# Seven block products for seven more pairs, and a setup that is split between two stages

## The chip, the cores and the metric

The kernel runs on one core of a Trainium2 chip. A core has five engines, each with its own instruction stream: PE (TensorE, matrix products), DVE (VectorE) and ACT (ScalarE) for elementwise work, POOL (GpSimd) and SP (SyncE), which mostly issue transfers here; ACT issues some too. Sixteen DMA engines move the data. The metric is device microseconds of one execution, the median of three runs. In the profile PE is the matmul stream and PEld the weight loads that run beside it.

## The reference

A trunk of two layers over 512 tokens with 1024 channels, all in float32. Each layer is: half a SwiGLU feed-forward, a token mixer, half a SwiGLU feed-forward, each behind an RMSNorm and with a residual. The mixer of the first layer is a chunked state-space scan (SSD), that of the second a diagonal state-space model (S5).

```python
def rmsnorm(x, g):
    xf = xf * lax.rsqrt(jnp.mean(xf * xf, axis=-1, keepdims=True) + NORM_EPS)
    return xf.astype(x.dtype) * g

def swiglu(h, w_in, w_out):            # FFN_DIM = 2816
    gate, up = jnp.split(h @ w_in, 2, axis=-1)
    return (jax.nn.silu(gate) * up) @ w_out

def s5_mixer(h, b_re, ..., glu_w, glu_b):
    step = jnp.exp(log_step)[:, None]
    lam_bar = jnp.exp(lam * step)                      # 64 groups x 64 complex states
    b_bar = ((lam_bar - 1.0) / lam)[..., None] * lax.complex(b_re, b_im)
    ...  # states[t] = lam_bar * states[t-1] + b_bar u[t];  y = Re(c states) + d u
    val, gate = jnp.split(gelu(y) @ glu_w + glu_b, 2, axis=-1)
    return val * jax.nn.sigmoid(gate)
```

So there are six stages in order: `f1_0`, `ssd`, `f2_0`, `f1_1`, `s5`, `f2_1`, and a final norm.

## The kernel before

The residual stream lies transposed in SBUF as eight tiles `xT[d]` of 128 channels by 512 tokens. Float32 accuracy comes from splitting each operand in a high and a low half (`H`, `L` of the activations, `whi`, `wlo` of the weights): a product is three matmuls, hi x hi, hi x lo and lo x hi (`proj`, L371 to L376). ACT casts the high half (L365), DVE subtracts for the low one (L367). Weights come through a ring of four staging tiles `wst` and rings of three `whi` and `wlo`.

**Feed-forward stages** (`ffn`, from L590). The 22 pairs of a gate and an up tile (128 hidden channels each) are worked in three parts, pairs 0 to 7, 8 to 14 and 15 to 21 (`PARTS`). Each part ends with eight output products, one for each `xT[d]`, which is updated at once. The norm's factor is applied to the products, so `H` and `L` hold the input times the gain.

A *plain* pair is two `proj` of eight k-steps with 512 columns. A *block* pair (class `Seven`, L385) uses a seven-product scheme for 2 x 2 blocks: the two halves of the tokens are the columns, and even and odd 128-channel tiles of the input together with gate and up give the blocks. It needs sums and differences of weight tiles, formed partly by accumulating DMAs on POOL's queue (L391, L392) and partly on DVE (L431, L435), and four *forms* of the activations (`forms`, L319, one call for each two input tiles), sums and differences of the scaled `xT` tiles, split in halves again. Each product is 4 k-steps x 3 matmuls of 256 columns, all at L445. Stages `f1_1` and `f2_1` use block pairs throughout, `f2_0` three plain pairs and then block pairs, `f1_0` only plain pairs.

**The S5 setup** (`s5_setup`, from L1051) has nothing to do with the data: it computes from the S5 parameters the operators `d_H` and `d_P`, and tables of rotation angles `d_t`, and leaves them in HBM for the S5 stage. It runs inside `f1_0`: `ffn` calls the next entry of a list `fill` after each pair and each output product (46 places). `lam` does the exponentials and powers in pieces, doubles the angle (`usq`), `tables(i)` builds eight tables of 8 groups each by doubling, `ops(i)` the operators of four groups, `ops_pe(i)` products on PE for two such steps. All its tiles lie in the pool `pre0`, freed when `f1_0` ends. Every table has 128 partitions, real and imaginary rows with a sign that differs between the two halves of the partitions.

**The order.** In `f1_0` all engines' orders come from a planner that simulates time; instructions inside `keep_in_program_order` keep their order among each other, and `issue_after(x)` puts those of a block behind `x`. In the other feed-forward stages PE keeps the written order (`manual_schedule(engines=MAN)`). `paced` is such a kept transfer on SP's queue. Each queue works strictly in order.

**The S5 stage** (`s5_stage`) loads per block of eight groups `U`, `opH`, `tb` (a table) and two `opP` tiles. The 16 `opP` tiles come through a ring of six (`hx`), loaded by SP at L1409. `swap_in` and `swap_out` exchange the two halves of the partitions on ACT. The gated product at the end (`glu_w`, `load_w` on POOL's queue) and the first block pairs of `f2_1` (`seven_ahead`) overlap the last scans.

## Time and profile before

| what | us |
|---|---|
| median of three runs (1981.59 to 1982.64) | 1982.21 |
| profiled execution | 1983.18 |
| its span | 1981.4 |
| PE busy | 1964.9 |
| DVE busy | 1524.8 |
| ACT busy | 944.7 |
| POOL busy | 237.1 |

The profiled execution's own time is 1.78 us more than the span that its instructions cover. The stages lie in the span at about 0 to 390 (`f1_0`), 390 to 807 (`ssd`), 807 to 1153 (`f2_0`), 1153 to 1496 (`f1_1`), 1496 to 1637 (`s5`) and from there to the end (`f2_1`). The granted clock is 0.999 of the full one. A row of a group reads: line, engine, operation, written tile <- read tiles, shapes, count | busy us, mean ns of one | idle time of the engine before them and what ended it. A row of the timeline or the chain begins with the start and the length in us.

### The profile page before, as it was taken

The numbers are of one execution on the slowest core, as the hardware profiler recorded it, in microseconds if no ns is written. First come the engines' busy times: TensorE is split into PE (matmuls) and PEld (weight loads), VectorE is DVE, ScalarE is ACT, GpSimd is POOL, SyncE is SP. The second block draws the span as 40 slices with busy tenths as digits, with TensorE's granted clock in tenths as the row PEclk, the third lists the DMA queues.
The fourth block names the chain that finished last, engine by engine and source line by source line (L and its number), as shares of the span: only waits on it lengthen the run. The fifth ranks groups of instructions, "written<-read, shape, count | busy, mean of one in ns | idle before, by whom it ended". The sixth has DMA issues, their size and how long they took to land.

```text
span 1981.4 us, 32556 instructions
## 1 busy us (share of the span) xinstructions
PE 1964.9 (99%) x12669; PEld 1735.2 (88%) x12669; DVE 1524.8 (77%) x2630; ACT 944.7 (48%) x1472; POOL 237.1 (12%) x261
## 2 busy tenths in 40 slices
PE   9999999999999999999999999999999999999998
PEld 7888888888888888898989899898988789999897
DVE  6898986888888678875858887585868668667685
ACT  5322233565565355552525555352557446435363
POOL 1000000012111110111202111120201112111110
PEclk9999999999999999999999999999999999999999
DMA  7444564544333422684858767585998348667572
GB/s 191 107 138 146 155 194 128 138 126 133 114 105 113 116 88 76 134 185 107 182 122 176 187 142 172 115 177 121 185 265 284 89 105 174 160 136 167 122 158 86
DMA packets 503994, 288.28 MB, mean 145 GB/s; under 512 B 47808, under 2 KB 489312, under 8 KB 503840
## 3 DMA queue, kind: packets, MB, share of 16 engines
q1 hardware_dynamic: 408384, 217.02, 38.7%
q0 software_dynamic: 73728, 55.28, 16.9%
q10 hardware_dynamic: 21728, 13.91, 2.5%
q8 instruction: 99, 1.62, 0.3%
q14 instruction: 55, 0.45, 0.1%
HBM read 264.60 MB, written 21.04 MB: 144 GB/s over the span
## 4 chain that ended last, share of the span: by engine, by line
PE 93%; DVE 3%; DMA 2%; ACT 1%; issue 1%; ACTq 0%; SPq 0%; DVEq 0%
PE mm L445 31%; PE mm L374 18%; PE mm L375 18%; PE mm L376 18%; DMA wst<-in_s_glu_w_dram 1%; PE aux L959 1%; PE aux L901 1%; PE aux L1564 1%; PE aux L951 0%; DMA xt<-in_x_dram 0%; PE aux L852 0%; PE aux L376 0%; PE aux L375 0%; PE aux L374 0%; DMA opP<-d_P 0%
## 5 line engine op out<-in xcount | busy, mean ns | idle before, releaser
L365 ACT CAST whi<-wst 128x1024 fp32r<-128x1024 f32 (+2 forms) x220 | 216.9, 991 | 412.7 <-PE mm L375 275.4
L374 PE MATMUL mm<-hH,whi 128*128 128x512 f32 x776 | 306.3, 395 | 0.0
L375 PE MATMUL mm<-hL,whi 128*128 128x512 f32 x776 | 302.4, 390 | 0.0
L376 PE MATMUL mm<-hH,wlo 128*128 128x512 f32 x776 | 302.4, 390 | 0.0
L445 PE MATMUL mm<-hx,whi 128*128 128x256 f32 x1512 | 280.8, 283 | 0.0
L367 DVE TENSOR_TENSOR wlo<-wst,whi 128x1024 fp32r<-128x1024 f32 (+2 forms) x220 | 253.7, 1155 | 29.2 <-ACT whi L365 27.2
L374 PE MATMUL mm<-ah,whi 128*128 128x512 f32 x648 | 252.7, 391 | 0.0
L375 PE MATMUL mm<-al,whi 128*128 128x512 f32 x648 | 252.5, 390 | 0.0
L376 PE MATMUL mm<-ah,wlo 128*128 128x512 f32 x648 | 251.9, 390 | 0.0
L445 PEld LDWEIGHTS mm<-hx,whi 128*128 128x128 f32 x1512 | 236.4, 192 | 0.7
L410 DVE TENSOR_TENSOR wlo<-wst,whi 128x1024 fp32r<-128x1024 f32 x126 | 154.3, 1224 | 91.8 <-ACT whi L407 88.7
L445 PE MATMUL mm<-hx,wlo 128*128 128x256 f32 x756 | 214.1, 283 | 0.2 <-DVE wlo L410 0.2
L445 PE MATMUL mm<-hL,whi 128*128 128x256 f32 x672 | 190.3, 283 | 0.5 <-DVE hL L272 0.3
L445 PE MATMUL mm<-hH,wlo 128*128 128x256 f32 x672 | 190.6, 284 | 0.2
L445 PE MATMUL mm<-hH,whi 128*128 128x256 f32 x672 | 190.3, 283 | 0.0
L376 PEld LDWEIGHTS mm<-hH,wlo 128*128 128x128 f32 x776 | 145.6, 188 | 30.6
L374 PEld LDWEIGHTS mm<-hH,whi 128*128 128x128 f32 x776 | 145.7, 188 | 30.4 <-issue 0.7
L375 PEld LDWEIGHTS mm<-hL,whi 128*128 128x128 f32 x776 | 145.8, 188 | 29.5 <-issue 0.2
L407 ACT CAST whi<-wst 128x1024 fp32r<-128x1024 f32 x126 | 131.6, 1045 | 37.3 <-PE mm L375 29.6
L445 PEld LDWEIGHTS mm<-hx,wlo 128*128 128x128 f32 x756 | 145.1, 192 | 0.4 <-DVE wlo L410 0.4
L376 PEld LDWEIGHTS mm<-ah,wlo 128*128 128x128 f32 x648 | 121.6, 188 | 25.3
L375 PEld LDWEIGHTS mm<-al,whi 128*128 128x128 f32 x648 | 121.7, 188 | 24.8 <-issue 0.4
(499 smaller groups left out, 3936.3 us busy)
## 6 DMA issues: line engine op xcount, KB each, us to landing
wst<-in_ffn_w_in_dram SPq DMA_DIRECT2D x175, 512.0 KB, 4.4
wst<-in_ffn_w_out_dram SPq DMA_DIRECT2D x56, 448.0 KB, 4.2
wst<-in_ssd_in_proj_dram SPq DMA_DIRECT2D x48, 512.0 KB, 3.9
wst<-in_ffn_w_out_dram SPq DMA_DIRECT2D x39, 512.0 KB, 4.1
wx<-in_ffn_w_in_dram SPq DMA_DIRECT2D x63, 256.0 KB, 3.2
wx<-in_ffn_w_in_dram POOLq DMA_DIRECT2D x63, 256.0 KB, 6.9
wst<-in_ffn_w_in_dram POOLq DMA_DIRECT2D x63, 256.0 KB, 5.0
dec<-d_cs POOLq DMA_DIRECT2D x16, 512.0 KB, 5.3
```

The costliest lines, as they stand in the source:

```text
L365: S.copy(hi, st)
L367: V.tensor_tensor(lo, st, hi.bitcast(F32), op=OP.subtract)
L374: PE.matmul(ps, hi[:, k], H[k], start=first and k == 0, stop=False)
L375: PE.matmul(ps, hi[:, k], L[k], start=False, stop=False)
L376: PE.matmul(ps, lo[:, k], H[k], start=False, stop=last and k == n - 1)
L407: self.pin(S.copy(hi, st))
L410: self.pin(V.tensor_tensor(lo[:, c], st[:, c], hi[:, c].bitcast(F32), op=OP.subtract))
L445: PE.matmul(ps, w_[:, j], b_, start=nm not in self.open, stop=False, skip_group_check=True)
L901: PE.matmul(pst[c], st["bt"][:, c * 128:(c + 1) * 128], st["wx"][:, c], start=True, stop=True)
L959: PE.matmul(py[e][hh * 64:(hh + 1) * 64, s], st["dtx"][:, c, k0:k0 + 64], M[:, hh, s], start=True, stop=True)
L1564: PE.matmul(py[i, h][e * 64:e * 64 + 64, g * 128:g * 128 + 128], l[:, h * 4 + g], out_ops(i + e, h)[:, g, w:w + 128], start=first and g == ...
```

## The change

1. **`f1_0`:** pairs 15 to 21 become block pairs. Since `xT` has been updated by then, `forms` gets a way (`split_only`) that adds the halves `H` and `L` again in place of reading `xT`. The four forms are made at output products 1 to 4 of the second part, the first block pair's transfers are issued at product 5 and its splits come at product 7. From pair 15 on, PE keeps the written order. The forms' tiles (pools `hx0`, `h10`) take the memory of the setup's pool, which is closed at output product 1.
2. **The setup in two parts:** in `f1_0` it is squeezed from 45 entries into 24 (pairs 0 to 14, the first eight output products and one more). The angle is left in a small tile `turn`. The doubling and the tables move to `f2_0` (`s5_tables`, 11 entries at places 4 to 35).
3. **Halved tables:** the angle tile holds 32 groups on each half of the partitions, so a table build makes two tables at once (four builds in place of eight, on half-width operands while doubling). Both halves of a stored table are the same now, written by four transfers on ACT's queue in place of one on POOL's; the sign goes into one of the two copies of `swap_in` and `swap_out`. The builds have two `t_cs` buffers.
4. **S5 tiles:** the last two `opP` tiles are loaded early, in kept order, into `wst` tiles; the first gated weight's transfer is issued early and its split held behind the last scan; the first block pairs of `f2_1` issue their transfers behind the last clearing of a state tile on POOL.
5. Some setup tiles share or leave tags (`p_E` takes the place of `p_B2` before it, `p_ks` its own), and the last `ks` stores go to POOL's queue.

```diff
-        def forms(self, j, fp, hp):
+        def forms(self, j, fp, hp, split_only=False):
...
+            if split_only:
+                he, le, ho, lo_ = [t_[i].bitcast(F32) for i in (e, o) for t_ in (self.H, self.L)]
+                V.tensor_tensor(a[:, lo], he[:, lo], le[:, lo], op=OP.add)
+                V.tensor_tensor(a[:, hi], a[:, lo], he[:, hi], op=OP.subtract)
+                V.tensor_tensor(a[:, hi], a[:, hi], le[:, hi], op=OP.subtract)
+                V.scalar_tensor_tensor(b[:, lo], ho[:, hi], -1.0, a[:, hi], op0=OP.mult, op1=OP.subtract)
+                V.tensor_tensor(b[:, lo], b[:, lo], lo_[:, hi], op=OP.subtract)
...
         for f in range(a, b):
             u.normed = normed
-            n = Seven(pr, w_in, f + 1, fp, pin) if f + 1 < b else None
+            with ExitStack() as behind:
+                if f == 0 and pr.after:
+                    behind.enter_context(tc.issue_after(pr.after.ins))
+                n = Seven(pr, w_in, f + 1, fp, pin) if f + 1 < b else None
...
+        if tail:
+            plain = PARTS[-1][0]
...
+                if tail and a == plain:
+                    seven = True
+                    by_hand.enter_context(tc.manual_schedule(engines=MAN))
...
+                    if tail and b == plain:
+                        if d == 1:
+                            hp = tail()
+                        if d in (1, 2, 3, 4):
+                            formed = pr.forms(d - 1, fp, hp, split_only=True)
+                        elif d == 5:
+                            u = Seven(pr, w_in, b, fp)
+                        elif d == KD - 1:
+                            with tc.issue_after(formed.ins):
+                                u = seven_first(pr, w_in, b, fp, u)
...
-            ER = pp.tile([128, 8, 64], F32, tag="p_wh", name="p_ER", bufs=2)
-            EI = pp.tile([128, 8, 64], F32, tag="p_wh", name="p_EI", bufs=2)
+            E_ = pp.tile([128, 2, 8, 64], F32, tag="p_B2", name="p_E", bufs=1)
+            ER, EI = E_[:, 0], E_[:, 1]
...
-            G.dma_start(d_t[i], cs)
...
-                nc.scalar.dma_start(ov[q, :, 4 * i:4 * i + 8, 128 + 16 * q:256], ks[:, :, 0:128 - 16 * q])
+                (G if i == 14 else nc.scalar).dma_start(ov[q, :, 4 * i:4 * i + 8, 128 + 16 * q:256], ks[:, :, 0:128 - 16 * q])
...
+        fill = [masks, both(rows, one, lambda: load_c(0), lambda: load_c(1)), both(one, lambda: load_c(2), b(0, 1)),
+                both(one, b(2, 3)), both(one, lambda: c_cols(0), b(4, 5)), both(one, lambda: c_cols(1), b(6, 7)),
+                both(one, lambda: c_cols(2), swap_b), both(steps.pop(0), lambda: c_cols(3), zero.pop(0))]
+        while steps:
+            f = steps.pop(0)
+            fill.append(both(f, zero.pop(0)) if zero and len(fill) % 2 else f)
+        assert not zero and len(fill) == 23
+        return fill + [lambda: ops_pe(14)]
+
+    def s5_tables(tp):
+        c, s = s5["turn"][:, 0], s5["turn"][:, 1]
...
+            for _ in range(3):
+                usq(c, s)
+            yield
+            for j in range(6):
+                V.tensor_copy(UC[:, j], c)
+                V.tensor_scalar(US[:, 0, j], s, -1.0, None, op0=OP.mult)
+                V.tensor_copy(US[:, 1, j], s)
+                if j < 5:
+                    usq(c, s)
+                if j == 2:
+                    yield
+            yield
+            for i in range(4):
+                cs = tp.tile([128, 2, 8, 64], F32, name="t_cs", bufs=2)
...
+                    if j == 3:
+                        yield
+                for h in range(2):
+                    for e in range(2):
+                        nc.scalar.dma_start(s5["t"][i + 4 * h][64 * e:64 * e + 64], cs[64 * h:64 * h + 64])
+                yield
...
     def out_ops(i, h):
         if (i, h) not in s5_out:
+            src = s5["P"][:, i * 8 + h * 4:i * 8 + h * 4 + 4]
+            if i >= KD - 2 and h:
+                P_ = wpool.tile([128, KD, 128], F32, name="wst", bufs=4).rearrange("p (g a) n -> p g (a n)", g=4)
+                paced(P_, src)
+            else:
...
-                    pin(S.copy(fl(z2)[64:128, c], p[0:64, c]))
+                    pin(S.activation(fl(z2)[64:128, c], p[0:64, c], AF.Copy, scale=-1.0))
...
                     if m == 2:
+                        for e in range(2):
+                            out_ops(KD - 2 + e, 1)
                         glu_k(0)
...
-            p0, w0 = aux_ps(), load_w(glu_cols(2 * NR), KD, eng=G)
+            p0, st0 = aux_ps(), fetch_w(glu_cols(2 * NR), KD, G)[0]
...
+            w0 = behind_states(split_w, st0, KD)
+            nxt.after = st[KD - 1]["cleared"]
...
                 if d == KD - 1 and nxt.kind == "wino":
-                    seven_ahead(nxt)
+                    with tc.issue_after(nxt.after.ins):
+                        seven_ahead(nxt)
...
+                    tabs, fill = s5_tables(tp), [lambda: None] * 46
+                    for n in (4, 10, 12, 14, 18, 20, 24, 26, 28, 33, 35):
+                        fill[n] = tabs.pop(0)
+                    ffn(pr, wi[L], wo[L], nxt, fill=fill, hp=hp)
```

161 lines of the change are left out of this document (85 added, 76 removed).

## The prediction

> **What bounds the kernel now.** I read the page's busy table and chain first, then windows by stage, then single rows.
>
> ```profile
> span 1981.4 us, 32556 instructions
> PE 1964.9 (99%) x12669; PEld 1735.2 (88%) x12669; DVE 1524.8 (77%) x2630; ACT 944.7 (48%) x1472; POOL 237.1 (12%) x261
> PE 93%; DVE 3%; DMA 2%; ACT 1%; issue 1%; ACTq 0%; SPq 0%; DVEq 0%
> ```
>
> TensorE never rests for long, and it carries 93% of the chain that ended last. So time leaves this kernel only where a TensorE instruction leaves its stream, or where one of the few idle gaps closes. All else decides only whether that gain is kept. DVE is the one to watch; the windows follow the first stage (0 to 390), its part before and after 268 us, the third stage (807 to 1149), and that stage's last seven pairs and last outputs. The columns are length, then busy time and count of PE, PE's weight loads, DVE, ACT and POOL, clock, DMA share and GB/s.
>
> ```profile
> 0.00:18.00 18.00, 15.56 (x84) 12.46 (x85) 9.87 (x25) 10.13 (x17) 9.00 (x24) 1.00 0.95 267
> 18.00:42.00 24.00, 24.00 (x140) 19.03 (x139) 17.89 (x39) 13.74 (x20) 0.18 (x1) 1.00 0.60 160
> 42.00:60.00 18.00, 18.00 (x81) 14.90 (x80) 11.60 (x18) 7.19 (x10) 0.00 (x0) 1.00 0.38 104
> 60.00:100.00 40.00, 40.00 (x179) 33.10 (x178) 36.99 (x128) 12.29 (x18) 0.00 (x0) 1.00 0.46 106
> 100.00:225.00 125.00, 125.00 (x573) 103.11 (x572) 115.63 (x339) 35.37 (x45) 3.77 (x7) 1.00 0.50 146
> 0.00:268.00 268.00, 265.56 (x1264) 217.44 (x1265) 228.15 (x606) 89.94 (x124) 13.48 (x33) 1.00 0.55 151
> 807.00:1149.00 342.00, 342.00 (x2326) 316.18 (x2325) 255.84 (x386) 164.78 (x247) 51.58 (x41) 1.00 0.68 152
> 1039.00:1109.00 70.00, 70.00 (x581) 69.87 (x580) 60.12 (x87) 39.94 (x61) 15.25 (x12) 1.00 0.80 169
> 1120.00:1150.00 30.00, 29.72 (x138) 24.73 (x137) 28.99 (x51) 19.19 (x33) 2.57 (x2) 1.00 0.51 121
> ```
>
> From 60 to 225 us DVE is busy 152.62 of 165 us (92.5%), yet TensorE waits for nothing. DVE can be driven that hard here without a stall.
>
> **Seven pairs as block products.** A plain pair is 2 x 8 x 3 = 48 matmuls of 512 columns; a block pair is 7 x 4 x 3 = 84 of 256 columns. The prices are two rows of the plain stream (51 matmuls apart) and one chain row of a whole block pair.
>
> ```profile
> 44.67 0.39 PE L376 MATMUL mm<-hH,wlo 128*128 128x512 f32 x1
> 56.23 0.39 PE L376 MATMUL mm<-hH,wlo 128*128 128x512 f32 x1
> 1877.35 10.08 PE mm L445 x84
> ```
>
> 11.56 / 51 = 0.2267 us, so a plain pair takes 10.88 us and a block pair 10.08. Seven pairs save 7 x 0.80 = **5.6 us** of stream. The output products stay as they are, so does the setup's TensorE work. The seam from plain to block pairs in the third stage costs nothing (342.00 of 342.00 busy); I allow 0.5 us for the new seam, whose weights and forms come later, between 0 and 1.
>
> The Trainium skill, "TensorE: Matmul & The Clock Gate", section "Back-to-back issue gap", gives 518 cycles for 512 columns and 262 for 256; at 2.4 GHz that would estimate 10.36 and 9.17 us a pair and a gain of 8.3 us. The same section says that the spacing in a stream is set by weight load and matmul together. "Perfetto Trace Analysis", section "Matmuls", prefers larger matmuls, which speaks against the change; the trace agrees in kind (two halves cost 0.240 us against 0.227).
>
> **Will DVE be ready for it?** The third part of the stage now needs 4 forms, made from the split halves, before its first block product that uses them. TensorE gets there at 263.46, plus the setup's products that used to come later (five groups at L1340, two times eight at L1330: 5 x 0.58 + 2 x 0.87 = 4.6 us): about 268.
>
> ```profile
> 263.46 0.39 PE L374 MATMUL mm<-hH,whi 128*128 128x512 f32 x1
> 361.23 0.87 PE aux L1330 x8
> 382.89 0.58 PE aux L1340 x16
> L1064 DVE TENSOR_TENSOR p_cs<-p_cs,p_tb 128x16 f32<-128x16 f32 (+5 forms) x48 | 16.0, 333 | 0.7
> ...
> L1064 DVE TENSOR_TENSOR p_cs<-p_cs,p_UC 128x16 f32<-128x16 f32 (+5 forms) x48 | 15.5, 332 | 0.5
> L1064 DVE TENSOR_TENSOR p_c<-p_c,p_den 128x64 f32<-128x64 f32 x8 | 1.8, 221 | 0.1
> L1064 DVE TENSOR_TENSOR p_G<-p_G,p_t 128x576 f32<-128x576 f32 x9 | 6.7, 749 | 0.1
> ...
> L1349 DVE SCALAR_TENSOR_TENSOR p_ks<-ident,p_dT,p_ks 16x16 f32<-16x16 f32 x40 | 6.5, 217 | 0.0
> ...
> L1064 DVE TENSOR_TENSOR p_Ht<-p_rER,p_B 128x512 f32<-128x512 f32 x8 | 5.5, 686 | 1.4 <-PE aux L1340 1.4
> L683 DVE SCALAR_TENSOR_TENSOR xT<-mm,xT 128x512 f32<-128x512 f32 x24 | 16.3, 685 | 10.2 <-PE mm L376 10.1
> L367 DVE TENSOR_TENSOR wlo<-wst,whi 128x896 fp32r<-128x896 f32 x6 | 6.4, 1085 | 0.1
> L329 DVE TENSOR_TENSOR hx<-ta,hx 128x256 fp32r<-128x256 f32 x4 | 1.7, 419 | 0.0
> L410 DVE TENSOR_TENSOR wlo<-wst,whi 128x1024 fp32r<-128x1024 f32 x40 | 49.0, 1224 | 26.5 <-ACT whi L407 25.8
> ```
>
> (The rows from p_G to p_Ht are the largest, one between and the smallest of seven, and count only what ran after 268.) Leaving DVE: the tables' three rows, 47.3, and the doubling of the angle, 8 x 8 operations at about 0.22 and 18 copies near 0.19: 17.4. Coming forward of 268: the seven rows, 43.7. New: a form is ten 256-column operations at 0.42 and one of 512 at 0.68, 4.9 us, four are 19.5; the first block pair's two weight splits and two sums, 2 x 1.22 + 2 x 0.69 = 3.8; four small copies, 0.5. Net 67.5 - 64.7 = +2.8 us on 228.15: **231 of 268 us**. At the 92.5% shown, 18 to 268 offers 231 beside the 9.9 before, so it fits with some 10 us over, if the setup starts in the holes of the first 60 us (12.5 us idle from 18 to 60): its first steps hang on earlier places of the list now.
>
> The forms also need memory which the setup's tiles hold, so they follow its end. Setup, less what comes after it (forms and splits 23.3, seven output steps at 1.09 + 0.69 = 1.8: 12), must be through: 231 - 35 = 196 us of DVE work. With the first 60 us as shown (39.4) and 92.5% after, that is reached at 60 + 156.6 / 0.925 = 229 us. The forms' 19.5 plus five output steps' 8.8 then end near 258, while their first reader (after two products, 2.9 us) comes at 271. **Cover 13 us, cost 0.** Behind it, a block pair costs DVE 60.12 / 70 = 86% of its time, as in the third stage, where TensorE is full: 0 again.
>
> **Tables in the third stage.** Half the tables, 23.7 us, and the doubling on half-width operands, at most 17.4: up to 41 us on DVE, against 342 - 255.8 = 86 idle. Most pieces sit at output steps; two (5.9 us) sit in the last seven pairs, where 9.9 of 70 are idle, ahead of a stretch with 29 of 30 busy. I take 0; at worst these 5.9 become a stall. The stores move from POOL's queue to ACT's: 16 issues.
>
> ```profile
> L1333 ACTq DMA_DIRECT2D d_H<-p_hs x4: 333/344/344, 362.6 to 382.8; - x4
> L464 ACT ACTIVATE up<-mm 128x256 f32<-128x256 f32 x19 | 7.3, 384 | 19.4 <-PE mm L445 19.4
> L459 ACT COPY gt<-mm 128x256 f32<-128x256 f32 x19 | 7.1, 373 | 42.4 <-PE mm L445 42.3
> ```
>
> 16 x 0.344 = 5.5 us of ACT, which idles 177 us there. An issue that waits for a late table holds the weight casts queued behind it; three weight buffers cover that, so 0, within the same 5.9. In the S5 stage copies become scaled copies: 11 ns each, nothing.
>
> **S5 tiles.** The last two output operators no longer wait for the ring that the products before them free; they are read into weight staging early.
>
> ```profile
> 1545.26 1.09 PE L1564 MATMUL aux<-opP,U 128*64 128x128 f32 x14 [1.25 <-DMA opP<-d_P]
> 1549.26 1.97 PE L1564 MATMUL aux<-opP,v 128*64 128x128 f32 x32
> 1566.95 0.39 PE L376 MATMUL aux<-gh,wlo 128*128 128x512 f32 x1
> wst<-in_s_glu_w_dram POOLq DMA_DIRECT2D x12, 512.0 KB, 4.8
> L365 ACT CAST whi<-wst 128x1024 fp32r<-128x1024 f32 (+2 forms) x220 | 216.9, 991 | 412.7 <-PE mm L375 275.4
> ```
>
> This 1.25 us gap closes. The two staging buffers come back when the products end, at 1551.2; a column load that has to wait for one lands 4.8 us later, 1556, and its cast and split take 0.99 + 1.22, so 1558, before the 1567 at which TensorE is done with the columns before it. Gain **1.25**, between 0 (another operator is late next) and 1.25.
>
> **Sum.** Against the profiled execution: span 1981.4 - 5.6 - 1.25 + 0.5 = 1975.05; 1.78 us lie around the span (1983.18 - 1981.4), and the median is 0.97 below that execution: 1975.05 + 1.78 - 0.97 = **1975.9 us**, about 6.3 us or 0.32% faster. What a measurement of this kernel can tell from no change is about 0.2%, 4 us.
>
> **Rivals.**
>
> A. *The setup's end holds the forms (slower).* Place: the turn from setup memory to forms, in the outputs before the last seven pairs. If setup frees its tiles at time t, the first reader waits t + 19.5 + 8.8 - 271: nothing up to t = 243, and slower than before by 4 us once that wait exceeds 6.3 + 4, from t = 253. For it: DVE has to sustain 92.5% for 170 us, TensorE goes over to the written order there, and eight stores of the last setup step go to POOL's queue ahead of the accumulating weight loads. Against: the 14 us between 229 and 243. At t = 258 the time is 1975.9 + 15 = 1991.
>
> B. *Gain half lost.* The same wait at t = 246 to 252, or the tables' 5.9 us in the third stage: 1979 to 1985, no change. For: those windows are the fullest of DVE; against: their pieces are bound to no place on DVE.
>
> C. *Operator wait only moves.* The first term alone: 1975.9 + 1.25 = 1977.2, still faster.
>
> D. *Half-width products at half price.* If 256 columns took half of 0.2267, a pair would save 10.88 - 9.52 = 1.36 and seven 9.5, giving 1972. The 10.08 row speaks against it. The skill's figures above point this way.
>
> **How the numbers follow.** Forecast 0.50 (own range 1974.5 to 1977), C 0.12, B 0.18, A 0.15, D 0.05. Faster by over 0.2% is the forecast, C and D: 0.67, less 0.02 for small mishaps: 0.65. Within: B and that, 0.20. Slower: 0.15. The range is 1973.5 to 1985: below lies D, above lies A.
>
> **What would show it.** Right: third part of the first stage from the first block product to the outputs in 70.6 us, no TensorE idle between 225 and 275, no wait on opP, third stage still 342 of 342. Wrong: TensorE idle at the first products on forms, released by DVE; idle near 1045 to 1150 behind a table or an ACT cast; or block products in the first stage spaced wider than 0.120 us.

## The result and the profile after

The changed kernel takes **1995.22 us** (1994.01 to 1997.58), the kernel before 1982.86 beside it: a ratio of **1.0065**, 95% interval 1.0054 to 1.0075. It is 12.4 us slower where 6.3 us faster was forecast, and well outside the range that ended at 1985. The profiled execution of after is the longest of its runs (1997.58, span 1995.8).

The page of after begins with the span, the busy time of each engine, and (part 4) each engine's share of the chain that ended last.

```profile
span 1995.8 us, 33202 instructions
PE 1966.3 (99%) x12921; PEld 1748.6 (88%) x12921; DVE 1542.6 (77%) x2646; ACT 966.9 (48%) x1519; POOL 262.8 (13%) x275
PE 92%; DVE 5%; DMA 1%; issue 1%; ACT 1%; ACTq 0%; DVEq 0%; SPq 0%
```

Shares over the whole span show little: DVE has 5% of the chain where it had 3%. The loss appears by stage. Both traces are cut here at the same PE instructions: the first block product of `f2_0`, that of `f1_1`, the first S5 product (`aux<-U,W`), and the first block product of `f2_1`.

| us | to `f2_0` | `f2_0` | `f1_1` | S5 | rest | span |
|---|---|---|---|---|---|---|
| before | 836.30 | 311.56 | 349.80 | 128.00 | 355.74 | 1981.4 |
| after | 835.36 | 321.33 | 348.85 | 134.35 | 355.91 | 1995.8 |
| difference | -0.94 | +9.77 | -0.95 | +6.35 | +0.17 | +14.4 |

Of the 5.6 us of the first column little is left, and two stages without a new product got longer. The list of what PE waited for (total, times, longest) names three places:

```profile
PE mm L459 <- DVE wlo L424: 8.2, 4, 3.8
PE aux L1564 <- issue: 4.0, 1, 4.0
PE aux L1650 <- DVE z L1581: 1.7, 1, 1.7
```

**First place, the new seam in `f1_0`.** The timeline of after ahead of the first block product and around it; in brackets the idle time ahead of a row and what ended it.

```profile
41.96 0.74 DVE L340 TENSOR_TENSOR ta<-hH,hL 128x256 f32<-128x256 f32 x2
...
248.25 1.54 DVE L1347 SCALAR_TENSOR_TENSOR p_ks<-ident,p_dT,p_ks 16x16 f32<-16x16 f32 x8 [0.87 <-ACT p_ks L1344]
...
254.79 0.95 ACT L379 CAST whi<-wst 128x896 fp32r<-128x896 f32 x1 [2.08 <-PE mm L389]
255.64 0.40 ACT L329 CAST h<-ta 128x256 fp32r<-128x256 f32 x1
...
261.53 0.76 DVE L340 TENSOR_TENSOR ta<-hH,hL 128x256 f32<-128x256 f32 x2
...
270.84 0.43 DVE L330 TENSOR_TENSOR hx<-ta,hx 128x256 fp32r<-128x256 f32 x1
271.18 1.23 DVE L424 TENSOR_TENSOR wlo<-wst,whi 128x1024 fp32r<-128x1024 f32 x1
...
272.46 0.39 PE L459 MATMUL mm<-hH,wlo 128*128 128x256 f32 x1 [3.42 <-DVE wlo L424]
```

The first two forms are summed early, from 41.96 on, and then occupy the two buffers for sums. The setup's last work on DVE is the row at 248.25. The splits of the two forms begin at 255.64, with casts on ACT behind a weight cast that had to wait for PE. Forms three and four need the same buffers, so they are summed and split only from 261.53 on, one DVE chain of ten microseconds. The first weight split is held behind the last of them (`issue_after(formed)`), and PE pauses for 3.42 us. The windows of after (length, then busy time and count of PE, weight loads, DVE, ACT and POOL, clock, DMA share, GB/s) show that it was not a lack of DVE time:

```profile
0.00:268.00 268.00, 265.65 (x1337) 216.27 (x1338) 225.62 (x492) 99.96 (x155) 18.70 (x37) 1.00 0.66 165
...
250.00:261.50 11.50, 11.50 (x52) 9.51 (x52) 6.68 (x11) 5.21 (x9) 5.57 (x9) 1.00 0.88 235
261.50:272.40 10.90, 7.54 (x35) 6.08 (x33) 10.45 (x27) 2.69 (x6) 2.58 (x2) 1.00 0.61 78
```

DVE idles 4.8 of the 11.5 us just ahead of the chain in which it is then full.

**Second place, the tables in `f2_0`.** The timeline of after at its largest pause there:

```profile
873.99 0.07 DVE L1408 MEMSET t_cs<- 128x8 f32 x1 [4.06 <-DMA d_t<-t_cs]
...
874.16 1.22 DVE L424 TENSOR_TENSOR wlo<-wst,whi 128x1024 fp32r<-128x1024 f32 x1
...
875.43 0.58 PE L459 MATMUL mm<-h,wlo 128*128 128x256 f32 x1 [3.79 <-DVE wlo L424]
```

The third table takes the first one's buffer, whose stores were still reading it. DVE waits 4.06 us in front of the memset, with a weight split queued behind it. By the list of places this build belongs to a later part of the stage; DVE's order is free there, and all four builds and their stores ran between 802 and 918 us. The clock is at 0.50 from 874.28 to 881.10. So the 9.77 us divide as follows: PE's pauses in the stage sum to 5.5 us more than before; the 5.67 us at half clock behind the large one cost about 2.8 (an estimate, half of them); some 1.4 are left.

**Third place, the S5 operators.** The DMA issues of 1519 to 1538 us in after (KB each, median us to landing), then the same stretch of the stage before (1511 to 1530):

```profile
DMA packets 2622, 6.14 MB, mean 323 GB/s; under 512 B 1188, under 2 KB 1188, under 8 KB 2620
...
opP<-d_P SPq DMA_DIRECT2D x4, 512.0 KB, 11.0
wst<-d_P SPq DMA_DIRECT2D x2, 512.0 KB, 12.6
wst<-in_s_glu_w_dram POOLq DMA_DIRECT2D x2, 512.0 KB, 12.5
tb<-d_t SPq DMA_DIRECT2D x2, 512.0 KB, 10.2
...
U<-d_u SPq DMA_DIRECT2D x2, 256.0 KB, 12.8
```

```profile
DMA packets 3551, 5.91 MB, mean 311 GB/s; under 512 B 2240, under 2 KB 2240, under 8 KB 3549
...
opP<-d_P SPq DMA_DIRECT2D x8, 512.0 KB, 6.3
tb<-d_t SPq DMA_DIRECT2D x3, 512.0 KB, 5.6
...
U<-d_u SPq DMA_DIRECT2D x2, 256.0 KB, 5.8
```

The engines move about as much in both, and their packets take 95% of the engines' time before and 97% after, so they were full before. Now the staged operators and the early gated weight, four transfers of 512 KB, compete with what the scans need next. All landings take about twice as long, and the issues themselves become slow, as timeline rows of after show (SP, DVE and PE):

```profile
1529.10 7.78 SPq L1448 DMA_DIRECT2D U<-d_u  x2
1536.98 3.77 SPq L1462 DMA_DIRECT2D tb<-d_t  x1
...
1537.89 0.66 PE L1650 MATMUL aux<-ident,gy 128*128 128x128 f32 x4 [1.71 <-DVE z L1581]
1541.78 0.69 DVE L1552 TENSOR_TENSOR U<-U,rL 128x512 f32<-128x512 f32 x1 [3.34 <-DMA U<-d_u]
1542.57 0.69 PE L1564 MATMUL aux<-U,opH 128*64 128x64 f32 x8 [4.02 <-issue]
```

The two `U` issues took 1.00 us before; here they hold SP's queue for 7.78, the table behind them is late, then `U` itself. The 4.02 us that the trace puts down to "issue" end as soon as `U` has been corrected on DVE.

### The profile page after: what moved, and what is told of

Read it like the earlier page. It is cut to its first block, busy times and chain, and to the rows that moved or that the text cites. A ratio compares the mean times of both kernels' runs of the same rounds, so it can differ in the third digit from the quotient of the medians.

```text
span 1995.8 us, 33202 instructions
## 1 busy us (share of the span) xinstructions
PE 1966.3 (99%) x12921; PEld 1748.6 (88%) x12921; DVE 1542.6 (77%) x2646; ACT 966.9 (48%) x1519; POOL 262.8 (13%) x275
## 4 chain that ended last, share of the span: by engine, by line
PE 92%; DVE 5%; DMA 1%; issue 1%; ACT 1%; ACTq 0%; DVEq 0%; SPq 0%
PE mm L459 33%; PE mm L388 17%; PE mm L389 17%; PE mm L390 17%; DVE wlo L424 1%; PE aux L993 1%; DMA tb<-d_t 1%; PE aux L935 1%; PE aux L985 0%; PE aux L1629 0%; PE aux L886 0%; PE aux L388 0%; PE aux L389 0%; PE aux L390 0%; DMA d_t<-t_cs 0%
## 5 line engine op out<-in xcount | busy, mean ns | idle before, releaser
L459 PE MATMUL mm<-hx,whi 128*128 128x256 f32 x1680 | 313.2, 284 | 0.0
L459 PEld LDWEIGHTS mm<-hx,whi 128*128 128x128 f32 x1680 | 263.8, 193 | 0.8
L388 PE MATMUL mm<-hH,whi 128*128 128x512 f32 x664 | 263.2, 396 | 0.0
L389 PE MATMUL mm<-hL,whi 128*128 128x512 f32 x664 | 259.0, 390 | 0.0
L390 PE MATMUL mm<-hH,wlo 128*128 128x512 f32 x664 | 258.8, 390 | 0.0
L459 PE MATMUL mm<-hx,wlo 128*128 128x256 f32 x840 | 238.4, 284 | 0.2 <-DVE wlo L424 0.2
L421 ACT CAST whi<-wst 128x1024 fp32r<-128x1024 f32 x140 | 146.3, 1045 | 37.2 <-PE mm L389 29.6
L405 POOL DMA_DIRECT2D wst<-in_ffn_w_in_dram x70 | 90.0, 1286 | 561.2 <-DVE p_Ht L1098 196.0
L406 POOL DMA_DIRECT2D wx<-in_ffn_w_in_dram x70 | 90.0, 1308 | 554.1 <-DMA wx<-in_ffn_w_in_dram 179.8
L390 PEld LDWEIGHTS mm<-hH,wlo 128*128 128x128 f32 x664 | 124.6, 188 | 26.2
L389 PEld LDWEIGHTS mm<-hL,whi 128*128 128x128 f32 x664 | 124.8, 188 | 25.0 <-issue 0.2
```

The lines of the kernel that those rows point to most:

```text
L388: PE.matmul(ps, hi[:, k], H[k], start=first and k == 0, stop=False)
L389: PE.matmul(ps, hi[:, k], L[k], start=False, stop=False)
L390: PE.matmul(ps, lo[:, k], H[k], start=False, stop=last and k == n - 1)
L405: G.dma_start(self.half(self.wu, 0), uo, accum_op=OP.add)
L406: G.dma_start(self.x[:, 0], ue, accum_op=OP.add)
L421: self.pin(S.copy(hi, st))
```

## The experiments

Where a run names one part, it is the changed kernel with that edit alone. Times by stage of their profiled executions, cut as above:

| run | median us | ratio (95%) | to `f2_0` | `f2_0` | `f1_1` | S5 |
|---|---|---|---|---|---|---|
| e1 three table buffers | 1993.12 | 1.0051 (1.0036 to 1.0066) | 835.79 | 317.64 | 348.82 | 133.16 |
| e2 operators in the ring | 1994.74 | 1.0061 (1.0046 to 1.0076) | 836.03 | 320.45 | 349.32 | 130.93 |
| e3 own memory for `p_E` | 1995.22 | 1.0063 (1.0046 to 1.0079) | 834.90 | 320.29 | 348.76 | 134.01 |
| e4 two `p_ks` | 1995.25 | 1.0066 (1.0051 to 1.0081) | 835.95 | 320.47 | 348.73 | 132.08 |
| e5 forms ahead | 1994.26 | 1.0063 (1.0048 to 1.0078) | 836.37 | 320.04 | 348.80 | 131.41 |
| e6 tables held in place | 2009.46 | 1.0138 (1.0123 to 1.0153) | 835.97 | 334.54 | 348.74 | 132.60 |
| e7 operators later | 1990.49 | 1.0045 (1.0028 to 1.0061) | 835.57 | 319.30 | 348.84 | 127.72 |
| e9 in place, stores later | 1995.44 | 1.0066 (1.0050 to 1.0081) | 834.73 | 319.37 | 350.27 | 132.90 |
| e10 buffers for the forms | 1989.86 | 1.0034 (1.0021 to 1.0046) | 830.82 | 320.41 | 348.76 | 132.74 |
| e11 = e7 + e9 + e10 | 1985.94 | 1.0016 (1.0007 to 1.0025) | 831.13 | 319.31 | 349.89 | 128.18 |
| e12 small pieces | 1986.33 | 1.0023 (1.0013 to 1.0033) | 830.39 | 320.01 | 350.46 | 127.31 |
| e13 builds on POOL | 1994.84 | 1.0058 (1.0043 to 1.0074) | 830.65 | 329.78 | 348.86 | 127.70 |
| e14 one table | 1983.92 | 1.0007 (0.9998 to 1.0016) | 830.60 | 316.80 | 349.72 | 128.20 |
| e15 = e12, stores on SP | **1978.20** | **0.9977** (0.9968 to 0.9986) | 830.76 | 313.01 | 348.77 | 127.10 |
| e16 = e12, stores on POOL | **1978.04** | **0.9979** (0.9969 to 0.9988) | 830.83 | 313.10 | 348.77 | 127.54 |
| e17 = e11, stores on SP | 1983.31 | 1.0002 (0.9994 to 1.0011) | 830.38 | 318.76 | 348.72 | 129.03 |
| e18 = after, stores on SP | 1995.03 | 1.0057 (1.0042 to 1.0073) | 835.75 | 320.74 | 348.74 | 133.30 |

Kernels with the changed S5 code left alone range from 131.41 to 134.35 in that stage, so a difference of one or two microseconds there says nothing.

### The seam in the first stage

**e3, own memory for `p_E`.** In after `p_E` shares `p_B2`'s memory and so delays the exchange of the operators; was that what made the setup late?

```diff
-            E_ = pp.tile([128, 2, 8, 64], F32, tag="p_B2", name="p_E", bufs=1)
-            ER, EI = E_[:, 0], E_[:, 1]
+            ER = pp.tile([128, 8, 64], F32, tag="p_wh", name="p_ER", bufs=2)
+            EI = pp.tile([128, 8, 64], F32, tag="p_wh", name="p_EI", bufs=2)
```

> In the setup, p_E gets back its own memory (that of p_wh, as before the change) and no longer lies in that of p_B2, so that the exchange of B's halves need not wait until p_E has been read at 106.87. Theory (late start): the setup's operators start some 10 us earlier, its end and the forms follow, TensorE's pause of 3.42 us at the first products on forms and the slow clock after it go: 4 to 6 us, total 1989 to 1991. Rival (late end): the casts of the first forms stand on ACT behind weight casts that wait for TensorE, whatever the setup does: the pause stays, 1994 to 1996.

The setup's last work on DVE ended some 2 us earlier, and the pause went from 3.42 to 2.96 us. The first column fell by 0.46 us, less than the spread of the kernels whose first stage is that of after (834.73 to 836.03). The total is the rival's.

**e4, two `p_ks`.**

```diff
-                    ks = pp.tile([16, 8, 128], F32, name="p_ks", bufs=1)
+                    ks = pp.tile([16, 8, 128], F32, tag=("p_ks", "p_crow")[i // 2 % 2], name="p_ks", bufs=1)
```

> The setup's tile p_ks alternates between two places in memory (its own and that of p_crow, which is free by then); every engine's order stays the same. Theory (late end): ACT's waits for the stores of p_ks (7.5, 8.7 us) go, the weight casts and the first forms' casts behind them come earlier, and TensorE's pause of 3.42 us shrinks to below 1.5: 3 to 5 us, total 1990 to 1992. Rival (late start, or DVE's volume): ACT's waits go, but the pause stays within 1 us: 1994 to 1996.

The pause stayed at 3.42 us. But ACT's waits for the `p_ks` stores did not go (the longest near the end 8.92 us, 8.71 in after), and the setup's last work on DVE ends at 250.1 as against 249.8. So this run does not tell whether the setup's end holds the forms.

**e5, forms ahead.** The forms' casts go ahead of the weight casts on ACT, and `p_hs` has memory of its own.

```diff
+                            if tail and b == plain and d >= 5:
+                                behind.enter_context(tc.issue_after(pr.first_cast.ins))
...
-                    hs = pp.tile([128, 4, 128], F32, tag="p_tA", name="p_hs", bufs=1)
+                    hs = pp.tile([128, 4, 128], F32, name="p_hs", bufs=1)
```

> The first two forms' casts on ACT are put ahead of the weight casts of output products 5 to 7 of the second part, and p_hs gets 2 KB of its own, so that the forms' memory is not held by its last store. Theory (order on ACT): at 251 to 255.6 the forms' casts stood behind two weight casts that waited for TensorE, with DVE idle and all forms behind them; put ahead, the forms are ready some 5 us earlier, and TensorE's pause of 3.42 us with the slow clock after it goes: 4 to 6 us, total 1989 to 1991.5. Rival (DVE's volume at the seam): the pause stays over 2.5 us: 1994 to 1996.

The pause moved ahead of the seam, as this timeline row of e5 shows: now an output product's weight split waited on DVE's queue. The forms' splits stood ahead of it, and ahead of these an `xT` update that waited for PE until 255.10.

```profile
260.06 0.79 PE L390 MATMUL mm<-ah,wlo 128*128 128x512 f32 x1 [4.09 <-DVE wlo L381]
```

So what counts is the order of forms and weights on ACT and DVE: advancing the forms' casts alone only delayed the weights.

**e10, buffers for the forms.** Forms three and four get the `gt` and `up` buffers, idle there; `p_E` and `p_hs` have their own memory, as in e3 and e5.

```diff
+            if split_only and j > 1:
+                a, b = [fp.tile([128, T], F32, tag=t_, name=nm) for t_, nm in (("gt", "ta"), ("up", "tb"))]
+            else:
```

> First stage only: the last two forms get buffers of their own while they are formed (those of gt and up, idle then), so that DVE can form them before the first two are split; p_hs has memory of its own, and p_E that of p_wh. Theory (DVE's work at the seam): 6 to 7 us of the forms' operations move from the full stretch of DVE at 261 to 271 into its idle time before 256, and TensorE's pause of 3.42 us with the slow clock after it goes: the first stage gains 4.5 to 5.5 us in place of 0.8, total 1989.5 to 1991.5. Rival (the splits follow the setup's end whatever is formed before): the pause stays over 2.5 us, 1994 to 1996.

The pause is gone and the first column is 830.82: 5.48 us below before and 4.54 below after. All four forms are now summed by 242.8, and their splits end at 267.3 in place of 271.2. The setup still ends its work on DVE at 249.7, so its end alone does not make the pause. The `p_E` part alone gained 0.46 (e3); the buffers without `p_hs`'s own memory were not tried, so how these two divide the rest stays open.

### The S5 operators

**e2, operators in the ring** (the staging undone):

```diff
-            if i >= KD - 2 and h:
+            if False:
```

> The last two output operators come through the ring of six again, as before the change; all else as after. Theory (transfers): the operators' 1 MB, and the gated weights that it pushes on, were put into a stretch in which the DMA engines were 90% busy, so the next table and the next U landed late; undone, the pauses of 1.71 and 4.02 us in the S5 stage and the slow clock after them go and the old gap of 1.25 us returns: S5 stage 4 to 5.5 us shorter, total 1989.5 to 1991. Rival (the other edits of the stage: scaled copies, orders behind the scan): nothing returns, 1994 to 1996.

The pauses of 1.71 and 4.02 us went, and S5 came to 130.93, 2.9 above before. That is only 0.5 below the lowest of the kernels named above, and the median is 1994.74, so by the total the rival's "nothing returns" holds. The trace shows what stands in their place: pauses of 1.01 and 0.77 us at the products on `opP`, where the kernel before paused for 1.25, and behind them 3.41 us at a clock of 0.50. By an estimate from these lengths that is 0.5 and 1.7 of the 2.9 us.

**e7, operators later:** the staging stays, but the two loads are asked for one block of groups later, behind the last `U`.

```diff
-                        for e in range(2):
-                            out_ops(KD - 2 + e, 1)
                         glu_k(0)
...
+                        for e in range(2):
+                            out_ops(KD - 2 + e, 1)
```

> The two staged operators are asked for one block later (behind the last two U transfers on SP's queue); all else as after. Theory (transfers): at that place their 1 MB no longer holds up U and the table, and they still come in time: the S5 stage from its first product to the first block product of the next stage (134.4 us after the change, 130.9 with the operators in the ring, 128.0 before) falls to 127 to 130, total 1989 to 1991. Rival (the gated weights issued early are what fills the DMA engines): 131 us or more, total 1993 or more.

S5 takes 127.72, and the old wait of 1.25 us for `opP` is gone as well. The other edits of this stage (the early gated weight, the block pairs' transfers) are all still in it, so they cost nothing that shows. What was wrong was the moment at which two loads were asked for.

### Pauses and the granted clock

**e8, six pauses:** the kernel before, with chains of VectorE work between two small PE products at six places of `f1_1`. It adds work and leaves out none, and was run once.

```diff
+                def pause(k):
+                    p = aux_ps()
+                    PE.matmul(p[:, 0:128], ident, ident, start=True, stop=True)
+                    t = work.tile([128, T], F32, tag="sq", name="pause")
...
+                    for _ in range(k):
+                        V.tensor_tensor(t, t, t, op=OP.mult)
+                    p = aux_ps()
+                    PE.matmul(p[:, 0:128], ident, t[:, 0:128], start=True, stop=True)
```

> The kernel before, with six TensorE pauses put into the fourth stage at output products, each made by a chain of DVE operations between two small products: 1, 2, 3, 4, 5 and 8 operations long, pauses of some 1.5 to 6 us. Theory (clock): a pause below about 3 us costs its own length and the granted clock stays at 1.00; one above about 3.4 us is followed by 3 to 6 us at 0.5 to 0.7, so that it costs 2 to 3.5 us more than its length. Rival: the low clock after the pauses of the changed kernel came with what made them, and the clock stays at 1.00 behind all six. Some 22 us in all by the theory, 18 or less by the rival.

The pauses came out at 5.23, 4.22, 3.90, 7.14, 6.26 and 7.53 us, 34.3 together, but the span grew from 1981.4 to 2031.5, by 50.1. Of the other 15.8 us at most 7.1 are the added products (six rows of 0.38 and six of up to 0.80 us); 9 to 16 are left, 1.5 to 2.6 us a pause. All six came out longer than planned, so the theory's first half, on pauses below 3 us, is not tested by this run; the rival fell. The windows behind the pause that ended at 1271.10 show them; the clock is the third number from the end:

```profile
1271.10:1273.00 1.90, 1.90 (x6) 1.61 (x7) 0.00 (x0) 0.00 (x0) 0.00 (x0) 0.50 1.19 195
1273.00:1275.00 2.00, 2.00 (x6) 1.61 (x5) 0.00 (x0) 0.00 (x0) 0.00 (x0) 0.50 0.59 177
1275.00:1277.00 2.00, 2.00 (x7) 1.53 (x7) 0.00 (x0) 0.00 (x0) 0.00 (x0) 0.59 0.00 0
1277.00:1280.00 3.00, 3.00 (x15) 2.47 (x14) 0.32 (x1) 0.54 (x1) 0.00 (x0) 1.00 0.00 0
```

### The tables in the third stage

**e1, three table buffers.**

```diff
-                cs = tp.tile([128, 2, 8, 64], F32, name="t_cs", bufs=2)
+                cs = tp.tile([128, 2, 8, 64], F32, name="t_cs", bufs=3)
```

> Three buffers for the tables in place of two; nothing else. Theory (store wait): the third table's first memset at 873.99 waited 4.06 us for the first table's store, and a weight split of the block pairs was queued behind it on DVE. With a third buffer TensorE's pause of 3.79 us near 875 and the slow clock after it (0.50 and 0.89 for some 10 us) go: third stage 8 to 9.5 us shorter, total 1985.5 to 1987.5. Rival (table volume): DVE has too much to do there whatever the buffers, the pause only moves by some us: 1993 to 1996.

The third table no longer waits, but the fourth does, 3.27 us, and PE pauses 2.98 us in place of 3.79. The stage gains 3.7 of its 9.8: 0.8 is the shorter pause, and most of the rest the clock, which stays at 1.00 behind this one (see the last section). The total lies in the rival's range.

**e6, tables held in place:** each piece is issued behind the last VectorE step of its place in the list.

```diff
-        n = lambda: next(gen)
+        def n():
+            with tc.issue_after(mark["v"].ins):
+                next(gen)
```

> Each of the eleven pieces of table work in the third stage is held on DVE behind the pair or output product at which it is listed; two buffers as after the change. Theory (tables pulled ahead): the planner had pulled all four builds into the first block pairs, and a memset waited for a buffer's store with weight splits queued behind it (4.06 us at 873.99 after the change, 3.27 us with three buffers, where it was the fourth table's); in their places no build waits for a store, and the pauses of 3.79, 0.74 and 0.53 us go: the stage, 321.3 us from its first block product to that of the next stage, falls to 311.6 to 314, total 1985.5 to 1988.5. Rival (volume): the bursts of table work delay weight splits wherever they stand: over 318 us, 1992 or more.

Much worse, and the reason is on ACT. Two rows of e6's timeline:

```profile
969.69 5.37 ACTq L1427 DMA_DIRECT2D d_t<-t_cs  x4
975.10 0.37 ACT L475 COPY gt<-mm 128x256 f32<-128x256 f32 x1 [9.36 <-issue]
```

The four stores wait for the table on ACT's queue, then take 1.3 us each, and the copy behind them, which PE needs, comes after 9.36 us of idle ACT; PE pauses 7.56 us.

**e9, stores later:** as e6, with each table's stores one place later, when it is finished, and each piece also behind the ACT cast of its place.

```diff
+                if i:
+                    store(i - 1, cs)
...
+            with tc.issue_after(mark["v"].ins), tc.issue_after(mark["a"].ins):
+                next(gen)
```

> Tables held in their listed places as in the run with tables in place, and each table's four stores put one place later on ACT, behind that pair's cast, so that no store waits on ACT's queue for a table still being built. Theory (stores on ACT): the pauses of 7.56 and 6.01 us there came from ACT, which had two weight casts and a product's copy queued behind stores that waited for the table; now neither these nor the memset's wait for a buffer (3.79 us after the change) are left, and the stage, 321.3 us after the change, falls to 311.6 to 314: total 1986 to 1988.5. Rival (bursts of table work on DVE stop the weight splits): pauses over 3 us stay and the total is over 1993.

No pause in the stage exceeds 1.7 us now, and it is still 7.8 us longer than before. The total did not move. `f1_1` now begins with two pauses of 0.75 and 0.77 us (350.27).

**e11, three repairs** (e7, e9 and e10 together):

> The three repairs together: tables in place with later stores, forms with buffers of their own, staged operators behind the last U. If each is worth what it is alone (about 8, 4.5 and 4.7 us of 1995.2) and nothing else stands behind them: 1977 to 1979, faster than before by some 4 us. Rival (the gain of the block pairs in the first stage is smaller than 7 x 0.80, or one repair's place is taken by another wait): 1981 to 1986, the same as before.

The first stage and S5 are mended, `f2_0` is not.

**e14, one table:** e11 with three of the four builds skipped.

> The three repairs together, with three of the four table builds left out: the first table is stored in the place of the others too, so tables 1 to 3 and 5 to 7 are wrong, and every store and every hold stays. Theory (table work on DVE is what the third stage still loses): some 18 of 39 us go, and the stage falls from 319.3 to 312 to 315.5 us, total 1979.5 to 1982.5. Rival (the stores on ACT, or the holds): it stays within 1.5 us of 319.3.

Work on DVE in the stage fell by 15 us (259.51 to 244.88), its time by 2.5 of the 7.75 us lost, which lies between the two expectations. So the amount of work counts for a part at most; e15 below keeps all of it.

**e13, builds on POOL.** On e7 and e10, the builds' elementwise steps move to POOL.

```diff
-                    tt(o, a_, bR, OP.mult)
+                    G.tensor_tensor(o, a_, bR, op=OP.mult)
```

> As the three repairs together, but with two buffers' order left to the planner as after the change, and the builds of the four tables (72 products and sums and the memsets) done by POOL in place of DVE; the angle stays on DVE. Theory (DVE): some 24 us leave DVE and no weight split stands behind a memset that waits for a store: the stage falls from 319.3 to 311.6 to 314 us, total 1978.5 to 1981.5. Rival (POOL): its operations hold up the accumulating weight loads on its queue, over 318 us.

The stage takes 329.78, with pauses of 3.62 and 4.21 us. Ahead of the first one the timeline of e13 has two DVE rows that run beside POOL's products:

```profile
866.20 3.34 DVE L489 TENSOR_TENSOR gt<-gt,rbc 128x512 f32<-128x512 f32 x1
869.46 3.15 DVE L427 TENSOR_TENSOR wlo<-wx,whi 128x1024 fp32r<-128x1024 f32 x1
```

Without POOL's products beside them, the same two operations take 0.69 and 1.22 us in this trace, and PE waits for the second. So DVE itself was slower beside POOL here. How much POOL's queued transfers add was not separated.

**e12, small pieces:** on e7 and e10, the eleven pieces become 32, at 24 places, mostly at output products.

```diff
+PLACES = ((5, 1), (8, 1), (9, 1), (10, 1), (11, 1), (12, 1), (13, 1), (14, 1), (16, 1), (18, 1), (20, 1), (23, 1), (24, 3), (25, 2),
+          (26, 1), (27, 3), (28, 2), (29, 1), (30, 2), (31, 1), (32, 1), (33, 1), (35, 1), (37, 2))
...
-                    if j == 3:
+                    if j in (1, 3, 4, 5):
                         yield
```

> As the three repairs together, but the table work of the third stage is cut into 24 small pieces (8 for the angle, four for each table) held at 24 places, mostly behind output products, where DVE idles 2.9 of 5.4 us, with the stores two places later. Theory (size of the pieces): with the whole volume kept, pieces of at most 2 us fit into what DVE has idle, the pauses of 0.7 to 1.3 us go, and the stage, 319.3 us with the three repairs and 311.6 before, falls to 312 to 315: total 1979 to 1982. Rival (DVE's volume in that stage as such): it stays over 317 us, total 1984 or more.

The total is as in e11, but the picture differs: PE has no pause up to 1036 us, and then one large one, by the waits, the timeline and two windows of e12:

```profile
PE mm L465 <- ACT gt L479: 4.1, 1, 4.1
```

```profile
1025.88 12.78 ACTq L1431 DMA_DIRECT2D d_t<-t_cs  x8
1038.77 1.04 ACT L427 CAST whi<-wx 128x1024 fp32r<-128x1024 f32 x1 [14.23 <-issue]
```

```profile
830.00:1036.06 206.06, 206.06 (x1395) 191.67 (x1393) 162.91 (x335) 86.07 (x124) 30.79 (x24) 1.00 0.69 155
1036.06:1150.40 114.34, 110.02 (x734) 102.33 (x733) 94.95 (x156) 61.03 (x95) 17.95 (x14) 0.97 0.78 178
```

Eight stores in a row hold ACT's queue for 12.78 us, 1.6 us an issue, and the weight cast behind them for 14.23. The pause of 4.08 us and the low clock behind it (a mean of 0.97 over 114.34 us, worth some 3 us by estimate) make about the 7 us by which e15 is shorter in this stage.

**e15 and e16, stores on another queue:** e12 with one word changed, SyncE (e15) or GpSimd (e16) in place of ScalarE.

```diff
-                        nc.scalar.dma_start(s5["t"][i + 4 * h][64 * e:64 * e + 64], cs[64 * h:64 * h + 64])
+                        nc.sync.dma_start(s5["t"][i + 4 * h][64 * e:64 * e + 64], cs[64 * h:64 * h + 64])
```

> The kernel of e12_small_pieces with one word changed: the sixteen table stores are issued on SyncE's queue instead of ScalarE's. If ScalarE's queue is what is left of the third stage's loss (eight stores in a row held its casts 14.23 us, TensorE paused 4.08 us), the stage, from the first second-stage block product of the feed-forward to the first plain product behind it, goes from 320.0 to 312-314.5 us, with no TensorE pause above 1 us in it, and the whole to 1977.5-1981 us, below the kernel before. Rival: the volume of VectorE's work or its extra instructions cost it, then the stage stays at 318 or more and the whole at 1984 or more.

> The same kernel with the table stores on GpSimd's queue. If it is only ScalarE's queue that mattered, the same gain as on SyncE's: stage 312-315 us, whole 1977.5-1982 us. Rival: any queue that holds eight stores in a row delays what stands behind it; on GpSimd's these are the accumulating output stores and the weight copies to BF16, then the stage stays at 317 or more, with a TensorE pause behind a GpSimd instruction.

Both come to 313 us in the stage and 1978 in all, **faster than the kernel before**; e16's rival about the length of POOL's queue fell. The stage's windows, of e15 and then of before:

```profile
830.76:1143.77 313.01, 312.77 (x2125) 291.03 (x2124) 259.50 (x494) 147.27 (x220) 48.73 (x38) 1.00 0.74 168
```

```profile
836.30:1147.86 311.56, 311.56 (x2126) 290.84 (x2124) 230.79 (x332) 147.74 (x220) 48.37 (x38) 1.00 0.69 155
```

DVE carries 28.7 us more and PE still rests only 0.24. Against e12 `f1_1` is 1.7 us shorter as well.

**e17 and e18, the queue alone:** the same word in e11, whose pieces are large, and in the changed kernel itself.

> The kernel of e11_three_repairs (table work in eleven large pieces, held at their places) with the stores on SyncE's queue. If the stores on ScalarE's queue alone cost the third stage, it goes from 319.31 to 312-314.5 us and the whole to 1978-1981.5 us, as in e15, whatever the size of the pieces. If the large pieces cost it by themselves (1.34 us behind a VectorE split, 0.94 behind ScalarE's casts), these pauses stay and the stage is at 316 or more, the whole at 1981.5-1985.

> The changed kernel with one word changed: table stores on SyncE's queue instead of ScalarE's. If ScalarE's queue alone cost the third stage, it goes from 321.3 to 312-315 us and the whole from 1995.2 to 1986-1989. If the wait of a table's memory for the stores that still read it (3.79 us pause) and the early pieces count too, that pause stays and the stage comes to 316-320, the whole to 1990-1994.

Neither stage recovers. In e17 the pauses behind ACT are gone, and those behind DVE stay:

```profile
PE mm L462 <- DVE wl L427: 4.0, 4, 1.3
```

In e18 the pause at the third table stays, 3.69 us, and the total is that of after. So once the pieces are held in place there are two causes, and either is enough. The stage's times, with the other repairs in:

| | stores on ACT | stores on SP |
|---|---|---|
| large pieces | 319.31 (e11) | 318.76 (e17) |
| small pieces | 320.01 (e12) | 313.01 (e15) |

The pauses over 0.3 us sum to 4 us in e17, against a loss of 5.75 to e15; the rest is in PE's busy time (314.45 against 312.77 for the same 2125 products) and has no row of its own. Large and small pieces also differ in the places at which they are held and in the moment of the stores, so the size alone is not shown to be the cause.

## Why the prediction was right or wrong

**Seven pairs, 5.6 us: right.** Where the seam is mended the first column gains 5.48 (e10) and 5.54 (e15). The chain of e15 has nearly the whole run of block products as one piece, 0.1204 us each, and no seam cost near the 0.5 us allowed:

```profile
269.73 69.33 PE mm L465 x576
```

**"Cover 13 us, cost 0": wrong, the first failed step.** The amount of DVE work was right (196 us forecast up to 229 and 194.94 measured; 231 up to 268 and 225.62 measured), and so, nearly, was the time of the first product on a form (271; 272.44 in e15). But the step took times from an amount of work at a mean rate, and both came late. The setup is through on DVE at 249.8, not at 229; what held it is not shown. "The forms then end near 258" did not follow the chain that makes a form: sums into one of two buffers, cast on ACT behind weight casts, split on DVE, and only then the next form. That chain ended at 271.2. It also held the first weight split, which is needed behind the first products at 268.64, before any form is read; the step did not price this hold. Cost 4.54 us by e10. The test written down for it, TensorE idle at the first products on forms, released by DVE, is nearly the row at 272.46, only that this product reads no form (`hH`) and waits for the weight split behind them. Rival A had the place, and its condition came true too (249.8 is past its 243). Its price did not follow: it gives a wait of 249.8 + 28.3 - 271 = 7 us where 3.42 was measured, and in e10, with the setup's end at 249.7, there is none.

**"I take 0; at worst these 5.9": wrong, the largest failed step.** The amounts were near enough (at most 41 us forecast, 32 measured in after and in e15, against 86 idle), as e15 shows by fitting them in at a cost of 1.45 us. The failed inference is that idle time on DVE can be filled wherever and by pieces of any size. In after the third build was pulled to 874 us, and its memset waited for the first table's stores, a wait not seen at all; the pauses and the low clock are some 8.4 of the 9.77 us. Rival B had counted it as a protection that the pieces "are bound to no place on DVE"; this freedom is what let the build come early. Holding large pieces in place did not help: they cost 5.75 us in e17 against the small ones of e15. The second error stands in "16 x 0.344 = 5.5 us of ACT": the price came from four issues of the setup; in after the median was 609 ns and the longest 1539. In after itself no pause of PE over 0.3 us in this stage ended on ACT; with the pieces in place the stores cost a pause of 7.56 us in e6, and in e12, where eight in a row took 12.78 us, "three weight buffers cover that" failed against a hold of 14.23. The place was also wrong: pauses were looked for at 1045 to 1150, and came at 875.

**"Gain 1.25, between 0 and 1.25": wrong, in sign.** The 1.25 us wait closed as described. But the step asked only when the buffers come back, and gave the two loads that it moved forward no price on SP's queue or on the DMA engines. Before, these engines already moved 311 GB/s in that stretch (323 after). Cost 6.35 us. In the eight kernels that ask for them one block later the stage takes 127.10 to 129.03 us, against 128.00 before and 126.63 in e8, whose S5 code is the same; so the loss is gone, and whether the 1.25 us are gained is not shown.

**A pause priced at its length: too low.** No term knew that PE's clock falls behind a pause. The windows of e8 show 0.50 for over 5 us after one of 4.22; the pauses in after are followed by 0.50 as well. The Trainium skill, "TensorE: Matmul & The Clock Gate", section "HAM oscillation — how this bites in real kernels", warns of idle gaps over about 3.4 us. The traces agree for six of six longer pauses in e8; below that length they show both (last section).

**The sum: near for the version in which the three failed steps are mended, and partly by luck.** Forecast was a span of 1975.05 us; e15's is 1975.5, though by other terms: -5.54, +1.45 in `f2_0`, -1.03 in `f1_1`, -0.90 in S5, +0.1 in the rest. Nothing in the forecast stands for the term in `f1_1`; 0.77 us of it is a wait of PE on ACT at 1493.61 in the trace of before, which e8, with the same code there, does not have. Its profiled execution took 1977.24 and its median is 1978.2, so the 0.97 us subtracted for the median did not hold, and the median is 2.3 us above the forecast of 1975.9.

**The rivals.** Three mishaps came at once, A's place with 4.54 us, the tables with 9.77 and S5 with 6.35. Each rival had only one of them at a time, and none had S5 as a loss, so the range stopped 10 us short. C and D fell: the operator wait closed in e7 and e15, and the products cost 0.1204, not half of 0.2267.

## What to carry to other kernels

Idle time of an engine is room only for pieces that fit, by place and size, between two of its instructions that the bound engine waits for, so follow that chain and its buffers instead of adding up busy time. A transfer that is asked for earlier takes its place from something: price it on the queue and on the DMA engines at the new moment, and keep runs of DMA issues off an engine whose queue also carries casts. When two causes can each hold a stage alone, removing one shows nothing (e12, e17), and only the pair of runs with both removed tells.

## What was not expected of the hardware

**The clock behind pauses.** A pause of 2.98 us in e1 was followed by the full clock, one of 2.96 us in e3 by half, and all six in e8, of 3.90 us and more, by half. The traces show what divides the two. Wherever the clock falls to 0.50 ahead of the end of a kernel, it stays there for 3.41 or 6.83 us (once 10.24, in e6), and within one trace these stretches begin whole multiples of 3.41 us apart. So each trace can be cut in steps of 3.41 us. Two steps of e1 around its pause, and then two of e3:

```profile
870.35:873.76 3.41, 1.72 (x15) 1.52 (x13) 0.15 (x3) 1.51 (x3) 0.00 (x0) 1.00 1.07 235
873.76:877.18 3.42, 2.13 (x17) 2.13 (x18) 3.42 (x8) 0.63 (x2) 0.48 (x1) 1.00 0.34 86
```

```profile
268.91:272.32 3.41, 0.52 (x4) 0.28 (x2) 3.08 (x6) 0.41 (x1) 0.00 (x0) 1.00 0.05 6
272.32:275.74 3.42, 3.35 (x15) 3.35 (x16) 2.53 (x4) 1.86 (x3) 0.00 (x0) 0.50 0.02 5
```

The pause in e1 is divided over two steps, and PE works 1.72 and 2.13 us in them; that in e3 lies in one, with 0.52 us of work, and the next step is at half clock. In all twenty traces, from 20 us on, each of the 56 steps at full clock in which PE idled 1.96 us or more was followed by 0.50, and none in which it idled less than 1.78; of the seven between, four were. Two short pauses in one step are enough (1.01 and 0.77 us in e2). The Trainium skill, "TensorE: Matmul & The Clock Gate", section "What's actually happening", says that the window in which activity is judged runs freely. The traces agree: against the start of the span the steps lie elsewhere in each of these two.

**The price of a DMA issue.** One form of store took 0.45 to 1.6 us on ACT's queue (e12) and 0.45 to 1.9 on SP's (e15), against 0.52 to 0.58 on POOL's (e16). The Trainium skill's first page, "Trainium Kernel Development and Optimization", section "Key Constraints", says that issuing from several engines only saves the sequencer's issue time, since all use the same 16 DMA engines; here the engine that spends it made the difference: 7 us between e12 and e15, in which ScalarE casts no longer wait behind it.
